# Low parts of the down-projection weights made by an accumulating DMA instead of a GpSimd subtraction

## The chip, the core and the metric

The kernel runs on one NeuronCore of a Trainium2 chip. The metric is the device time of one execution in microseconds (us); for several runs the median is given. TensorE is called PE, VectorE DVE, ScalarE ACT, GpSimd POOL or Pool, and SyncE, which issues the DMAs of before, SP.

## The reference

One layer of a hybrid diffusion backbone is computed for 512 latent tokens and 128 context tokens, 640 columns in all. The part that matters here is the last one, the down projection of the gated feed-forward network:

```python
f_gate, f_val = jnp.split(up, 2, axis=-1)
f = (jax.nn.silu(f_gate) * f_val) @ prm["w_ffn_down"]
x = x + g2 * rms_norm(f, prm["norm_ffn_post"])
```

`w_ffn_down` is 2816 x 1024 in float32. Ahead of it stand the mixing sub-layer (input projection, state-space scan, convolutions, output projection) and the up projection with its depthwise convolution.

## The kernel before

**Products in two parts.** A float32 product is made of three matmuls on rounded operands (fp32r). Each weight tile `raw` is split into a high part `hi`, which is `raw` rounded, and a low part `lo = raw - hi`; activations are split in the same way. `mm3` (L407 to L415) then adds hi x high, hi x low and lo x high. For each 128 x 128 block of weights PE so runs six matmuls, three products in two column halves of 384 and 256.

**Units.** The weights are cut into units of 128 x 1024 or less, one per load. `fetch` (L277) loads a unit with a DMA on SP's queue into `wr` (two buffers) and calls `split_unit` (L294). There the rounding `raw` to `wh` runs on ACT (L311) and the subtraction to `wl` on Pool or DVE (L313); `wh` and `wl` have three buffers each. So a unit's two parts can be written once PE is done with the unit three places earlier, and its raw buffer is free for the load two places later once the split has read it.

**The down projection.** Output block m (0 to 7, 128 rows each) needs three units g = 0, 1, 2 over the 2816 input rows; the third is 768 wide. `DOWN_ORDER` loads them as (0,0), (0,1), (1,0), (1,1), (0,2), (1,2), and from m = 2 on three by three: 24 units, called D0 to D23 in this order. Blocks 0 and 1 run interleaved, since the last activations are not yet there. Their splits (`split_act`, L397 to L404) go on at the same time: rounding on ACT (L400), subtraction on DVE or Pool (L402). The convolutions of the last up blocks on DVE (L1237 to L1240) and their gating product on Pool (L1339) run beside them. When a block is done, ACT squares and scales it (L1412, L1418) and Pool adds the square up (L1414). At the end the sums of squares give the norm, which is applied half by half on DVE and Pool (L1446, L1447) and stored.

**The order of the work.** The order in which each engine issues its instructions is written out by hand in the table `ORDER`, by positions in program order, and `issue_in_order` pins it. Engines issue strictly in that order and wait on semaphores, so a late operand holds up all that stands behind its reader on that engine. PE's order puts the first blocks of D2 among the last of D1.

Of the kernel before, what the change touches and what calls it, by code (L numbers as in the profile page):

```python
# [7 lines left out]
F32 = mybir.dt.float32  # L8
F32R = mybir.dt.float32r
AF = mybir.ActivationFunctionType  # L10
ALU = mybir.AluOpType
MUL, ADD, SUB, MAX, MIN = ALU.mult, ALU.add, ALU.subtract, ALU.max, ALU.min
# [25 lines left out]
for _name, _w in (("b_ada", 48), ("g_mix_pre", 8), ("g_mix_post", 8), ("g_ffn_pre", 8),  # L38
# [94 lines left out]
630 628-629 635 631 641 636-637 646 642 653 647-648 655 654 658 656-657 660 659 663 661-662 665 664 668  # L133
666-667 670 669 673 671 675 672 674 678 676 680 677 679 683 681 685 682 684 688 686 690 687 689 693 691 695
692 694 698 696 700 697 699 703 701 727 705 702 704 708 706 709 707 714 710-713 715 719 716 725-726 717 720
731 718 723 721-722 732 724 728-729 733-734 730 735 741 736-740 745 742-744 746-747 751 748-750 752-753 757
754-756 758-759 763 760-762 764-765 769 766-768 770-771 775 772-774 776-784""",
    "Pool": """
0-13 16-19 14-15 24-25 20 26-27 33 21-23 65 69 28-30 35 70 36 34 75 51 93 31 37-42 32 49 43 50 44-48 71 97
52-59 98 64 66 72 67 77 60 76 61 73 62-63 74 80 103-104 99 78-79 81-84 92 68 105 100 85-88 94 89 123 108 90  # L140
# [43 lines left out]
def hybrid_layer_kernel(ctx: ExitStack, tc: tile.TileContext, xT, ct, prm, cst, wrest, wdt, idhl_d, wada1, wada2, win,  # L184
                        wout, wup, wdown, st0, yT, nsf, nsb):
    nc = tc.nc
    te, ve, ac, gp, sy = nc.tensor, nc.vector, nc.scalar, nc.gpsimd, nc.sync
# [22 lines left out]
    def slot(tag, dt=F32, shape=(P, T)):  # L210
        if tag in ("H8", "T8"):
            return sb.tile([P, T + 64], dt, tag=tag, name=nm(tag))[:, 48:48 + shape[1]]
        return sb.tile(list(shape), dt, tag=tag, name=nm(tag))
# [55 lines left out]
    def add_unit(src, lo_eng=gp):  # L269
        units.append((src, lo_eng))  # L270
        return len(units) - 1
# [7 lines left out]
    def fetch(upto):  # L279
        if horizon[0] is not None:  # L280
            upto = min(upto, horizon[0])
        while cursor[0] < len(units) and cursor[0] <= upto:
            j = cursor[0]
            src, _ = units[j]
            n = src.shape[1]
            t = wp.tile([P, 1024], F32, tag="wr", name=f"wr{j}", bufs=2)
            sy.dma_start(t[:, :n], src)
            loaded[j] = t
            cursor[0] += 1
            split_unit(j)  # L290
# [5 lines left out]
    def split_unit(j):  # L296
        src, lo_eng = units[j]
        n = src.shape[1]
        raw = loaded.pop(j)
        if j in KEEP:  # L300
            parts = [[], []]
            for i, (c0, c1) in enumerate(((0, T), (T, n))):
                hi, lo = (slot(KEEP[j][2 * q + i], F32R, (P, c1 - c0)) for q in range(2))
                ac.activation(hi, raw[:, c0:c1], AF.Copy)
                lo_eng.tensor_tensor(lo, raw[:, c0:c1], hi.bitcast(F32), SUB)
                parts[0] += [hi[:, c:c + P] for c in range(0, c1 - c0, P)]
                parts[1] += [lo[:, c:c + P] for c in range(0, c1 - c0, P)]
            ready[j] = parts
            return
        hi = wp.tile([P, 1024], F32R, tag="wh", name=f"wh{j}")  # L310
        ac.activation(hi[:, :n], raw[:, :n], AF.Copy)  # L311
        lo = wp.tile([P, 1024], F32R, tag="wl", name=f"wl{j}")
        lo_eng.tensor_tensor(lo[:, :n], raw[:, :n], hi[:, :n].bitcast(F32), SUB)  # L313
        ready[j] = (hi, lo)


    unit_of = {}
# [70 lines left out]
    DOWN_ORDER = [(m, g) for gs in ((0, 1), (2,)) for m in range(2) for g in gs]  # L388
    DOWN_ORDER += [(m, g) for m in range(2, KD) for g in range(3)]
    for m, g in DOWN_ORDER:  # L390
        unit_of["down", m, g] = add_unit(wdown[m, :, 1024 * g:min(1024 * (g + 1), DFF)])


    split_ins = [None]
# [3 lines left out]
    def split_act(hi_tag, lo_tag, src, lo_eng):  # L398
        hi = slot(hi_tag, F32R)
        hi_ins[0] = ac.activation(hi, src, AF.Copy)  # L400
        lo = slot(lo_tag, F32R)
        split_ins[0] = lo_eng.tensor_tensor(lo, src, hi.bitcast(F32), SUB)  # L402
        return hi, lo
# [121 lines left out]
    for s in range(4):  # L525
# [6 lines left out]
        for k in (k0, k0 + 1):  # L532
# [3 lines left out]
            hi, lo = split_act(f"H{k}", f"H{8 + k}", xs_[k], ve)  # L536
# [390 lines left out]
    for it in seq:  # L927
        if it[0] == "proj":
            n = it[1]
# [7 lines left out]
            elif n[0] == "B":  # L937
                g = int(n[1:])
                bT[g] = slot("M2")
                conv3_silu(pt, 8 + g, bT[g])  # L940
            elif n[0] == "C":
                g = int(n[1:])
# [521 lines left out]
    m = KD - 1  # L1464
# [132 lines left out]
```

## Time and profile before

| what | us |
|---|---|
| median of 3 runs (lowest, highest) | 981.96 (980.89, 983.74) |
| span of the profiled execution, first to last instruction | 979.4 |
| PE busy | 944.5 |
| DVE busy | 686.9 |
| POOL busy | 577.9 |
| ACT busy | 471.3 |
| subtractions of weights on Pool (L313), 127 in all | 290.4 |
| roundings of weights on ACT (L311), 131 in all | 131.3 |

The profile is of one execution. Its span is 2.56 us below the median of the runs; the record gives no other time for that execution. Busy time is a sum over the span, whatever the engine held up. In the rows of the timeline the columns are start, length, engine, line, operation, output from inputs and count, and in brackets the idle time ahead of it with what ended it. A low part appears as `wl`, a high part as `wh`, a raw unit as `wr`. Rows that the prediction uses are shown there.

### The profile page before, as it was taken

To read this page: it belongs to the slowest core of one execution; us is meant where nothing else is said; L and a number is where in the kernel's file an instruction comes from. 1 tells how busy PE (TensorE), PEld (TensorE's weight loads), DVE (VectorE), ACT (ScalarE), POOL (GpSimd) and SP (SyncE) were. 2 spreads that over 40 slices of the span, in tenths; PEclk is the share of its full clock that TensorE was granted. 3 is DMA by queue.
4 is the path that set the end of the run, shared out by engine and by line. 5 is a ranking of instruction groups with operands and counts; after the bars stand their busy time and mean duration, and the time that the engine had idled before them with its cause. 6 is when DMAs were issued, how large, how long until landed. Compare 5 with 4: busy or idle time off the path is not lost.

```text
span 979.4 us, 18795 instructions
## 1 busy us (share of the span) xinstructions
PE 944.5 (96%) x7623; PEld 920.9 (94%) x7623; DVE 686.9 (70%) x1076; ACT 471.3 (48%) x799; POOL 577.9 (59%) x416
## 2 busy tenths in 40 slices
PE   4999999999999999999999999999999999999995
PEld 3799999999999998998889999999999999999995
DVE  1769898999989997523585998998988898400004
ACT  4355666877668477622464852323232336322211
POOL 1334699889999882534662994444454436543434
PEclk9999999999999999999999999999999999999998
DMA  9622424433424422578662322222222231322213
GB/s 347 250 72 86 117 82 127 146 95 123 139 80 142 128 91 93 196 244 303 200 218 88 129 86 69 84 78 73 86 66 86 66 87 54 94 69 76 82 38 108
DMA packets 50294, 117.52 MB, mean 120 GB/s; under 512 B 6016, under 2 KB 13952, under 8 KB 50208
## 3 DMA queue, kind: packets, MB, share of 16 engines
q1 hardware_dynamic: 50208, 116.33, 37.2%
q8 instruction: 60, 0.98, 0.4%
q14 instruction: 26, 0.21, 0.1%
HBM read 112.55 MB, written 3.75 MB: 119 GB/s over the span
## 4 chain that ended last, share of the span: by engine, by line
PE 87%; DMA 3%; ACT 3%; DVE 2%; SPq 1%; POOL 1%; issue 1%; POOLq 0%; ACTq 0%; DVEq 0%
PE ps L415 72%; PE ps L1259 3%; PE pq L415 2%; PE pq L818 2%; PE pq L807 1%; PE pq L460 1%; SPq L452 1%; DMA wr<-in_wout 1%; PE pq L744 1%; PE pq L441 1%; POOL wl L313 1%; PE pq L473 1%; DMA S<-acD 1%; ACT wh L311 1%; DMA T<-in_wada 1%
## 5 line engine op out<-in xcount | busy, mean ns | idle before, releaser
L313 POOL TENSOR_TENSOR wl<-wr,wh 128x1024 fp32r<-128x1024 f32 (+3 forms) x127 | 290.4, 2290 | 316.3 <-ACT wh L311 299.2
L415 PE MATMUL ps<-H,wh 128*128 128x384 f32 (+1 forms) x1636 | 315.7, 309 | 0.1
L311 ACT ACTIVATE wh<-wr 128x1024 fp32r<-128x1024 f32 (+3 forms) x131 | 131.3, 1003 | 316.2 <-PE ps L415 183.2
L415 PE MATMUL ps<-T,wh 128*128 128x384 f32 (+1 forms) x1472 | 272.5, 306 | 1.8 <-ACT S L1227 1.8
L1237 DVE SCALAR_TENSOR_TENSOR S<-ps,prms,S 128x441 f32<-128x441 f32 (+2 forms) x336 | 233.5, 695 | 29.4 <-ACT S L1227 18.9
L415 PEld LDWEIGHTS ps<-H,wh 128*128 128x128 f32 x1636 | 249.0, 188 | 2.7 <-issue 1.7
L415 PEld LDWEIGHTS ps<-T,wh 128*128 128x128 f32 x1472 | 218.9, 188 | 2.2 <-ACT S L1227 2.1
L872 DVE SCALAR_TENSOR_TENSOR ps<-u,prms,ps 128x655 f32<-128x655 f32 x205 | 185.1, 903 | 10.8 <-ACT ps L869 4.8
L415 PE MATMUL ps<-H,wl 128*128 128x384 f32 (+1 forms) x818 | 191.8, 309 | 0.0
L415 PE MATMUL ps<-T,wl 128*128 128x384 f32 (+1 forms) x736 | 166.2, 305 | 0.0
L415 PEld LDWEIGHTS ps<-H,wl 128*128 128x128 f32 x818 | 129.0, 188 | 1.0 <-issue 1.0
L415 PEld LDWEIGHTS ps<-T,wl 128*128 128x128 f32 x736 | 113.0, 188 | 0.0
L488 DVE RECIPROCAL rsm<-rsm 128x160 f32<-128x160 f32 (+2 forms) x9 | 7.4, 817 | 147.1 <-ACT rsm L487 147.1
L415 PE MATMUL ps<-S,wh 128*128 128x384 f32 (+1 forms) x420 | 88.0, 310 | 1.6 <-ACT wh L311 1.6
L415 PEld LDWEIGHTS ps<-S,wh 128*128 128x128 f32 x420 | 66.5, 188 | 2.8 <-ACT wh L311 1.8
L415 PE MATMUL ps<-S,wl 128*128 128x384 f32 (+1 forms) x210 | 54.9, 309 | 0.3 <-POOL wl L313 0.3
L789 ACT ACTIVATE S<-S,AC 128x128 f32<-128x128 f32 x140 | 45.5, 392 | 2.4 <-DMA S<-acD 2.4
L885 POOL TENSOR_TENSOR T<-T,T 128x640 f32<-128x640 f32 x20 | 32.0, 1602 | 12.5 <-ACT T L881 12.5
L1227 ACT ACTIVATE S<-ps,prms 128x640 f32<-128x640 f32 x42 | 36.5, 869 | 0.0
L415 PEld LDWEIGHTS ps<-S,wl 128*128 128x128 f32 x210 | 35.2, 188 | 0.9 <-POOL wl L313 0.5
L881 ACT ACTIVATE T<-u,prms 128x512 f32<-128x512 f32 (+1 forms) x54 | 27.9, 554 | 6.8 <-POOL T L885 6.8
L1339 POOL TENSOR_TENSOR H<-S,S 128x640 f32<-128x640 f32 x16 | 25.3, 1581 | 0.0
(346 smaller groups left out, 1180.3 us busy)
## 6 DMA issues: line engine op xcount, KB each, us to landing
wr<-in_wup SPq DMA_DIRECT2D x44, 512.0 KB, 3.5
wr<-in_win SPq DMA_DIRECT2D x36, 512.0 KB, 3.9
T<-in_wada SPq DMA_DIRECT2D x49, 256.0 KB, 5.4
S<-acD SPq DMA_DIRECT2D x28, 320.0 KB, 4.7
wr<-in_wdown SPq DMA_DIRECT2D x16, 512.0 KB, 3.4
wr<-in_wout SPq DMA_DIRECT2D x13, 512.0 KB, 4.5
H<-in_wada SPq DMA_DIRECT2D x23, 256.0 KB, 4.6
S<-in_wada SPq DMA_DIRECT2D x16, 256.0 KB, 5.4
```

The source lines that it names most:

```text
L311: ac.activation(hi[:, :n], raw[:, :n], AF.Copy)
L313: lo_eng.tensor_tensor(lo[:, :n], raw[:, :n], hi[:, :n].bitcast(F32), SUB)
L415: last_mm[0] = te.matmul(out, w, x[:, c0:c1], start=first and i == 0, stop=last and i == 2)
L789: ac.activation(rc, rc, AF.Relu, scale=-1.0, bias=AC2[:, c, row:row + 1])
L818: te.matmul(py[64 * h:64 * h + 64, i * P:(i + 1) * P], xt[:, c * P + 64 * h:c * P + 64 * h + 64], rs[h, d][:, c * P:(c + 1) * P], start=d ...
L872: ve.scalar_tensor_tensor(acc, u[:, j:j + UO], w(j), acc, MUL, ADD)
L881: ac.activation(t[:, b:c], u[:, a:a + c - b], AF.Copy, scale=w(j))
L885: gp.tensor_tensor(far, far, t, ADD)
L1227: ac.activation(out, v, AF.Identity, bias=prm_col("ffn_b", i), scale=w(1, 1))
L1237: ve.scalar_tensor_tensor(ob, vl[:, r0 + a - 1:r1 + a - 1, q0 + b - 1:q1 + b - 1], w(a, b), ob, MUL, ADD)
L1259: te.matmul(pt[:, o:o + c1 - c0], w[k] if i in (1, 2) else w[:, k * P:(k + 1) * P], x[:, c0:c1], start=k == 0 and j == 0, stop=k == KD - 1 ...
L1339: gp.tensor_tensor(f_raw[q], a, b, MUL)
```

## The change

For 22 of the 24 down units, all but D0 and D1, the low part is no longer a subtraction. ACT writes the negated rounding of the raw unit into `wl` (scale -1, output fp32r), and then a DMA issued from Pool's queue reads the raw weights from DRAM once more and adds them onto `wl` in place: -hi + raw. The high part, the raw load and PE's instructions stay as they are.

```diff
         lo = wp.tile([P, 1024], F32R, tag="wl", name=f"wl{j}")
-        lo_eng.tensor_tensor(lo[:, :n], raw[:, :n], hi[:, :n].bitcast(F32), SUB)
+        if j in ADDED:
+            ac.activation(lo[:, :n], raw[:, :n], AF.Copy, scale=-1.0)
+            gp.dma_start(lo[:, :n], src, accum_op=ADD)
+        else:
+            lo_eng.tensor_tensor(lo[:, :n], raw[:, :n], hi[:, :n].bitcast(F32), SUB)
         ready[j] = (hi, lo)
...
         unit_of["down", m, g] = add_unit(wdown[m, :, 1024 * g:min(1024 * (g + 1), DFF)])
+    ADDED = {unit_of["down", m, g] for m, g in DOWN_ORDER[2:]}
...
-731 718 723 721-722 732 724 728-729 733-734 730 735 741 736-740 745 742-744 746-747 751 748-750 752-753 757
+731-732 718 723 721-722 733-734 724 728-729 735-738 730 739-740 746-747 741-745 751-752 748-750 753-756
```

Of `ORDER` only ACT's list changes, where 22 instructions are put in; the last two lines of the diff are the place where that begins. The order of PE, DVE and SP is the same instruction by instruction.

ACT's queue around D2 and D3, before. Here `wh_9342` is the high part of D2 and `wr_9340` its raw unit, `wh_9396` that of D3; `T_814`, `H_820` and `H_822` are high parts of activations, `S_824` is the start of the last convolution and `S_807` the last gate:

```order
L311 ACTIVATE wh_9342<-wr_9340 128x1024
L400 ACTIVATE T_814_9275<-H_751_7890 128x640
L1227 ACTIVATE S_824_9295<-ps_798_9186,prms 128x640
L400 ACTIVATE H_820_9287<-H_766_8301 128x640
L400 ACTIVATE H_822_9291<-H_771_8438 128x640
L311 ACTIVATE wh_9396<-wr_9394 128x1024
L1333 ACTIVATE S_807_9251<-S_807_9251 128x640
```

The same place of ACT's queue with the change; `wl_9344` and `wl_9399` are the low parts of D2 and D3:

```order
L312 ACTIVATE wh_9342<-wr_9340 128x1024
L315 ACTIVATE wl_9344<-wr_9340 128x1024
L406 ACTIVATE T_814_9275<-H_751_7890 128x640
L1233 ACTIVATE S_824_9295<-ps_798_9186,prms 128x640
L406 ACTIVATE H_820_9287<-H_766_8301 128x640
L406 ACTIVATE H_822_9291<-H_771_8438 128x640
L312 ACTIVATE wh_9397<-wr_9395 128x1024
L315 ACTIVATE wl_9399<-wr_9395 128x1024
L1339 ACTIVATE S_807_9251<-S_807_9251 128x640
```

Each negated copy stands right behind the rounding of its unit, and everything behind it moves back by one instruction.

Pool's queue at the same place, before; `T_811`, `T_813` and `T_815` are low parts of activations, `S_825` is the last gating product, and `wl_9344`, `wl_9398`, `wl_9452`, `wl_9506`, `wl_9560` are the low parts of D2 to D6:

```order
L402 TENSOR_TENSOR T_811_9269<-H_737_7604,T_810_9267 128x640
L402 TENSOR_TENSOR T_813_9273<-H_746_7753,T_812_9271 128x640
L313 TENSOR_TENSOR wl_9344<-wr_9340,wh_9342 128x1024
L402 TENSOR_TENSOR T_815_9277<-H_751_7890,T_814_9275 128x640
L313 TENSOR_TENSOR wl_9398<-wr_9394,wh_9396 128x1024
L313 TENSOR_TENSOR wl_9452<-wr_9448,wh_9450 128x768
L1339 TENSOR_TENSOR S_825_9308<-S_807_9251,S_824_9295 128x640
L313 TENSOR_TENSOR wl_9506<-wr_9502,wh_9504 128x768
L313 TENSOR_TENSOR wl_9560<-wr_9556,wh_9558 128x1024
```

With the change:

```order
L408 TENSOR_TENSOR T_811_9269<-H_737_7604,T_810_9267 128x640
L408 TENSOR_TENSOR T_813_9273<-H_746_7753,T_812_9271 128x640
L316 DMA wl_9344<-in_wdown 128x1024
L408 TENSOR_TENSOR T_815_9277<-H_751_7890,T_814_9275 128x640
L316 DMA wl_9399<-in_wdown 128x1024
L316 DMA wl_9454<-in_wdown 128x768
L1345 TENSOR_TENSOR S_825_9308<-S_807_9251,S_824_9295 128x640
L316 DMA wl_9509<-in_wdown 128x768
L316 DMA wl_9564<-in_wdown 128x1024
```

Each subtraction is replaced by a DMA issue in the same place of the queue; nothing else on Pool moves. A DMA of this kind waits for ACT's negated copy, and the first matmul that reads the low part waits for the DMA where it waited for Pool.

More of the change, by code (lines that the diff above doesn't have):

```diff
@@ L135 @@
 692 694 698 696 700 697 699 703 701 727 705 702 704 708 706 709 707 714 710-713 715 719 716 725-726 717 720
-731 718 723 721-722 732 724 728-729 733-734 730 735 741 736-740 745 742-744 746-747 751 748-750 752-753 757
-754-756 758-759 763 760-762 764-765 769 766-768 770-771 775 772-774 776-784""",
+731-732 718 723 721-722 733-734 724 728-729 735-738 730 739-740 746-747 741-745 751-752 748-750 753-756
+760-761 757-759 762-765 769-770 766-768 771-774 778-779 775-777 780-783 787-788 784-786 789-792 796-797
+793-795 798-806""",
     "Pool": """
```

## The prediction

> **What bounds the kernel now.** I read the page first, then busy time by stage, then who waits for whom at the down projection, then the timelines of the four engines around the first changed unit. A change in the down units can only act on the stage that uses them, so the stages come before the totals.
>
> ```profile
> PE 944.5 (96%) x7623; PEld 920.9 (94%) x7623; DVE 686.9 (70%) x1076; ACT 471.3 (48%) x799; POOL 577.9 (59%) x416
> ...
> PE 87%; DMA 3%; ACT 3%; DVE 2%; SPq 1%; POOL 1%; issue 1%; POOLq 0%; ACTq 0%; DVEq 0%
> ```
>
> TensorE is busy in 96% of the span and carries 87% of the chain that ended last. The stages (columns: length; busy us of PE, PEld, DVE, ACT, POOL; granted clock; DMA share; GB/s):
>
> ```profile
> 806.00:846.00 40.00, 40.00 (x280) 40.00 (x279) 32.99 (x39) 19.86 (x27) 24.94 (x12) 1.00 0.23 68
> 846.00:962.00 116.00, 116.00 (x819) 115.72 (x818) 0.75 (x1) 29.54 (x44) 46.91 (x23) 1.00 0.23 66
> 962.00:979.40 17.40, 7.33 (x67) 6.83 (x65) 10.87 (x21) 2.01 (x6) 12.05 (x12) 0.78 0.43 152
> ```
>
> From 806 to 962 us, which is the whole down projection, PE has no idle time at a granted clock of 1.00. From 780 us to the end the view of waits, cut to PE, has only these, both in the tail behind the down units:
>
> ```profile
> PE pq L481 <- DVE rsm L488: 1.5, 1, 1.5
> PE pq L473 <- ACT AT L1412: 0.5, 1, 0.5
> ```
>
> So PE never waits for a low part here, and what the change removes from Pool cannot shorten the stage: its gain is 0. What remains is whether the new path delivers each low part before PE asks for it.
>
> **The change part by part.** I call the down units D0 to D23 in load order: (0,0), (0,1), (1,0), (1,1), (0,2), (1,2), (2,0), (2,1), (2,2), (3,0) and so on; those of the third column group are 768 wide. D2 to D23 are changed: 14 wide ones and 8 narrow ones.
>
> *Removed:* 22 Pool subtractions, from 806 to 962 us in these groups:
>
> ```profile
> L313 POOL TENSOR_TENSOR wl<-wr,wh 128x1024 fp32r<-128x1024 f32 x15 | 36.8, 2454 | 50.9 <-ACT wh L311 50.8
> L313 POOL TENSOR_TENSOR wl<-wr,wh 128x768 fp32r<-128x768 f32 x8 | 15.5, 1933 | 19.9 <-ACT wh L311 19.9
> ```
>
> 14 x 2.45 + 8 x 1.93 = 49.8 us of Pool work go, all of it beside a full PE: 0 us.
>
> *Added on ACT:* 22 negated copies of the shape of the rounding, 1.05 us wide and 0.85 us narrow (rows below), 14 x 1.05 + 8 x 0.85 = 21.5 us on an engine that is busy for 29.54 of 116 us. The cover is ACT's idle time; it is missing only where ACT is full, and that is at D2:
>
> ```profile
> 818.71 1.05 ACT L311 ACTIVATE wh<-wr 128x1024 fp32r<-128x1024 f32 x1
> 819.66 0.72 ACT L400 ACTIVATE T<-H 128x640 fp32r<-128x640 f32 x1
> 820.29 0.87 ACT L1227 ACTIVATE S<-ps,prms 128x640 f32<-128x640 f32 x1
> 821.06 1.36 ACT L400 ACTIVATE H<-H 128x640 fp32r<-128x640 f32 x2
> ```
>
> The negated copy stands right behind the rounding of D2, so it runs from 819.66 to 819.66 + 1.05 = 820.71, and the three rows behind it come 0.95 us later. The DVE shows whether that hurts:
>
> ```profile
> 821.32 7.49 DVE L402 TENSOR_TENSOR H<-H,H 128x640 fp32r<-128x640 f32 x4
> 828.73 5.80 DVE L1237 SCALAR_TENSOR_TENSOR S<-ps,prms,S 128x441 f32<-128x441 f32 x8
> ```
>
> The last convolution starts at 828.73, and its seed (ACT at 820.29) would be written at 822.1: 6.6 us to spare. The split halves that ACT delays (821.06) feed the third and fourth of the four DVE operations. Cost 0.
>
> *Added on Pool:* 22 DMA issues in the places of the subtractions. D2's stands between three activation splits and a fourth:
>
> ```profile
> 815.12 4.71 POOL L402 TENSOR_TENSOR T<-H,T 128x640 fp32r<-128x640 f32 x3 [3.03 <-ACT T L400]
> 819.89 2.42 POOL L313 TENSOR_TENSOR wl<-wr,wh 128x1024 fp32r<-128x1024 f32 x1
> 822.26 2.17 POOL L402 TENSOR_TENSOR T<-H,T 128x640 fp32r<-128x640 f32 x1
> ```
>
> Pool is free at 819.83, before the copy is done at 820.71, so Pool's queue adds no wait. The fourth split waits behind the issue as it did behind the subtraction. Now the reader of D2's low part, in PE's queue:
>
> ```profile
> 822.84 0.62 PE L415 MATMUL ps<-S,wh 128*128 128x384 f32 x3
> ...
> 824.16 0.27 PE L415 MATMUL ps<-S,wh 128*128 128x256 f32 x1
> 824.27 0.46 PE L415 MATMUL ps<-S,wl 128*128 128x384 f32 x2
> ```
>
> Before, the low part is ready at 819.89 + 2.42 = 822.31, and PE reads it at 824.27: 1.96 us of slack. Afterwards it is ready at 820.71 + L, where L runs from the end of the negated copy to the landing of the accumulating DMA. PE's queue is in order and every later matmul stands behind this one, so the whole kernel slips by 820.71 + L - 824.27 = **L - 3.56 us**. Nothing gives it back, since PE is full to 962 us.
>
> *L* has no row: before, no DMA is issued from Pool. The nearest rows (queue, count, KB each, median us to landing, then SP's own time for an issue in ns and the landing's minimum, median and maximum):
>
> ```profile
> wr<-in_wdown SPq DMA_DIRECT2D x16, 512.0 KB, 3.4
> ...
> wr<-in_wdown SPq DMA_DIRECT2D x8, 384.0 KB, 3.1
> ...
> H<-acD SPq DMA_DIRECT2D x4, 320.0 KB, 5.8
> ```
>
> ```profile
> L287 SPq DMA_DIRECT2D wr<-in_wdown x24: 327/328/328, 789.9 to 938.1; - x24
> ...
> DMA to landing us min/median/max: 3.0/3.4/4.1
> ```
>
> - the plain load of the same weights: 3.4 us;
> - the accumulation also has to fetch what lies in wl: one more 512 KB, at (3.4 - 3.1) us per 128 KB = 1.2 us;
> - the end of the same copy also frees the raw buffer, so SP loads D4 (384 KB) in the same moments: 3 x 0.3 = 0.9 us of shared engines;
> - Pool's own issue, between SP's 0.33 us and the 2.42 us of the subtraction in its place: I take the middle, 1.4 us.
>
> L = 3.4 + 1.2 + 0.9 + 1.4 = 6.9 us, and the stall at D2 is 6.9 - 3.56 = **3.3 us**. Low end: the fastest landing and SP's issue, 3.0 + 0.33 = 3.3 us, below 3.56: no stall. High end: the slowest load row of a similar size, 5.8, with the other terms at their highest, 5.8 + 1.2 + 0.9 + 2.4 = 10.3 us: 6.8 us at D2.
>
> [...]
>
> *Later units.* A buffer is freed three units earlier, so they have more room. The tightest, D6, and the first of the regular ones, D9 (rounding on ACT, then PE's first read of the low part):
>
> ```profile
> 841.83 1.04 ACT L311 ACTIVATE wh<-wr 128x1024 fp32r<-128x1024 f32 x1
> ...
> 859.00 1.06 ACT L311 ACTIVATE wh<-wr 128x1024 fp32r<-128x1024 f32 x1 [4.89 <-PE ps L415]
> ```
>
> ```profile
> 852.44 0.45 PE L415 MATMUL ps<-S,wl 128*128 128x384 f32 x2
> ```
>
> ```profile
> 871.40 0.45 PE L415 MATMUL ps<-S,wl 128*128 128x384 f32 x2
> ```
>
> With 2.0 us for the two ACT passes, D6 has 852.44 - 841.83 - 2.0 = 8.6 us for L, D9 has 871.40 - 859.00 - 2.0 = 10.4. At L = 6.9 neither stalls; at 10.3, D6 adds 1.7 us. Pool's sums of squares (six in the stage) stand in the queue where they stood and keep the same waits.
>
> **Sum.** The span of 979.4 plus 3.3 is 982.7 us. The median of the runs, 981.96, lies 2.6 us above the profiled span; with that, the forecast is **985.3 us**, 0.34% slower. About 0.3%, 2.95 us here, is what a measurement of this kernel can tell from no change; that is L = 6.5 us.
>
> **The rivals.**
>
> *Quick landing (0.37), no change to be measured.* If L stays under 6.5, the stall is 0 to 2.9 us: 982.0 to 984.9, around 983.5. For it: the down loads land within 3.0 to 4.1 us, and the stage's DMA share is 0.23, so there is room. Against it: it needs the second fetch, the neighbour load and Pool's issue together to stay under 3.1 us over the plain 3.4.
>
> *The accumulating DMA is slow by itself (0.12), slower by far.* If adding in flight stretches L past 10.4 us, the buffer ring no longer covers it and every output block pays. The deciding point is D9's room. At L = 12: 8.4 at D2, 3.4 at D6, then 1.6 in each of the five blocks 3 to 7, 8.0; together 19.8 us, 1001.8. No row speaks for such a rate, and none excludes it.
>
> *VectorE holds Pool's issue back (0.05), slower.* Pool and DVE disturb each other here:
>
> ```profile
> L402 DVE TENSOR_TENSOR H<-H,H x5: 812/2198/3032, 821.3 to 835.8; 128x640 fp32r<-128x640 f32 x5
> ```
>
> The same DVE subtraction takes 812 or 3032 ns. If the issue had to wait until the four at 821.32 are through (4 x 0.81 us undisturbed, to 824.6), L counts from there: 824.6 + 6.9 - 3.56 - 820.71 = 7.2 us, 989.2. [...]
>
> *Faster (0.04).* No wait of PE on a low part exists in the stage to be removed, and the order of instructions shows 22 real DMA issues, so the change does what it says. What is left is the spread of the runs, 980.89 to 983.74.
>
> **How the numbers follow.** The forecast, one stall of 2.9 to about 8.5 us, has 0.42. Slower by over 0.3%: 0.42 + 0.12 + 0.05 = 0.59; within 0.3%: 0.37; faster: 0.04. The range starts at 981.5 (no stall, less the spread) and ends at 991.0, just above the high end of L (979.4 + 6.8 + 1.7 + 2.6 = 990.5). It leaves out the slow accumulation (0.12) above and some 0.08 below.
>
> **What would show it.** In the profile after: one PE wait of about 3 us near 824 us on the DMA that writes wl, no other PE wait up to the tail, PE matmul time unchanged, Pool's subtractions down by 22 and its issues landing in about 7 us. No such wait would speak for the quick landing; waits at D6 and in every block from 3 on for the slow accumulation; an issue on Pool that begins only when the DVE run ends for the third. The prediction is wrong if the stage gets shorter, or if PE first waits elsewhere.

## The result and the profile after

The kernel with the change takes 988.88 us (median of 4 runs, 987.49 to 989.71); the kernel before, run beside it, 982.85 us (4 runs, 980.89 to 984.12). The ratio is 1.0063 with a 95% interval of 1.0045 to 1.0080: 6.2 us slower, between 4.4 and 7.9. Forecast were 985.3 us, between 981.5 and 991.0, and 3.3 us of loss.

The profiled execution after took 989.71 us, with a span of 987.9. From its page, the busy times:

```profile
PE 948.0 (96%) x7623; PEld 923.7 (94%) x7623; DVE 681.8 (69%) x1076; ACT 490.4 (50%) x821; POOL 545.0 (55%) x416
```

ACT is busy for 19.1 us more, the 22 copies, and Pool for 32.9 us less, the subtractions against the issues; neither is what the time shows. By stage (columns as in the prediction: length; busy us of PE, PEld, DVE, ACT, POOL; granted clock; DMA share; GB/s):

```profile
806.00:846.00 40.00, 36.65 (x246) 36.45 (x245) 30.05 (x44) 22.16 (x30) 16.95 (x12) 0.96 0.41 92
846.00:970.00 124.00, 124.00 (x874) 123.72 (x873) 1.02 (x2) 46.33 (x63) 25.16 (x24) 1.00 0.67 141
```

Before, the first of these stages had 40.00 us of PE at a clock of 1.00. Now 3.35 us of PE are missing in it, and the clock is 0.96; the second stage is full at 1.00 as before. The view of waits, PE alone, from 780 to 990 us, names the one new wait, beside the two of the tail that were there before:

```profile
PE ps L421 <- DMA wl<-in_wdown: 3.3, 1, 3.3
```

The three timelines around it, ACT with D2's negated copy, then Pool with D2's issue, then PE:

```profile
823.13 1.04 ACT L315 ACTIVATE wl<-wr 128x1024 fp32r<-128x1024 f32 x1
```

```profile
824.82 1.04 POOL L316 DMA_DIRECT2D wl<-in_wdown  x1 [1.51 <-ACT T L406]
```

```profile
827.64 0.27 PE L421 MATMUL ps<-S,wh 128*128 128x256 f32 x1
831.26 0.90 PE L421 MATMUL ps<-S,wl 128*128 128x384 f32 x2 [3.35 <-DMA wl<-in_wdown]
831.96 1.27 PE L421 MATMUL ps<-S,wh 128*128 128x384 f32 x4
...
833.56 1.06 PE L421 MATMUL ps<-S,wh 128*128 128x384 f32 x4
834.46 0.45 PE L421 MATMUL ps<-S,wl 128*128 128x384 f32 x2
834.74 0.73 PE L421 MATMUL ps<-S,wh 128*128 128x384 f32 x4
835.32 0.45 PE L421 MATMUL ps<-S,wl 128*128 128x384 f32 x2
```

The negated copy ends at 824.17, Pool's instruction starts at 824.82, and PE goes on at 831.26: from the copy to PE it is 7.1 us, against 3.56 that D2 had. Behind the wait six matmuls take 833.56 - 831.96 = 1.60 us instead of 835.32 - 834.46 = 0.86 a little later. The clock in steps of 2 us says why:

```profile
828.00:830.00 2.00, 0.00 (x0) 0.00 (x0) 2.00 (x4) 2.00 (x4) 0.71 (x1) 1.00 1.02 184
830.00:832.00 2.00, 0.74 (x3) 0.74 (x4) 1.89 (x4) 0.61 (x1) 0.16 (x1) 0.71 1.04 254
832.00:834.00 2.00, 2.00 (x9) 2.00 (x9) 1.90 (x4) 0.00 (x0) 0.00 (x0) 0.50 0.83 152
834.00:836.00 2.00, 2.00 (x15) 2.00 (x14) 1.93 (x5) 0.00 (x0) 0.00 (x0) 0.94 0.40 78
```

The granted clock is 0.50 from about 830.8 to 834.2. The 14 matmuls from 831.26 to 834.74 took 3.48 us; at 0.86 us for six they take 2.0. So the wait of 3.35 us brought 1.5 us of slow matmuls with it, 4.85 us in all.

The two profiled spans differ by 979.4 to 987.9, 8.5 us, more than that. The last matmul ahead of the wait shows the rest: it starts at 824.16 before and at 827.64 after, 3.48 us later, and up to D2's copy the queues hold the same instructions in the same order in both kernels. That part is not the change's. Almost half of it lies at 458.8 us, far ahead of the down projection, where the granted clock fell in the profiled execution of after and did not in that of before. The same stretch, before and then after:

```profile
458.00:463.00 5.00, 5.00 (x70) 4.54 (x62) 3.23 (x3) 2.05 (x4) 2.65 (x2) 1.00 0.81 277
```

```profile
458.00:463.00 5.00, 4.79 (x77) 4.12 (x78) 2.10 (x2) 2.16 (x4) 1.57 (x1) 0.66 0.90 293
```

That is 5.0 x 0.34 = 1.7 us of clock. Another 1.47 us lie between 22 and 30 us, where the clock of after was at 0.50 from 25.28 to 28.69 us (1.00 in the same stretch before) and PE waited 0.98 us for a DMA in place of 0.41: the matmul `pq<-csts,adar` at 22.23 us starts 0.02 us ahead of the same one at 22.25 before, the next of its kind at 29.94 us 1.45 behind that at 28.49. Some 0.3 us are left for small differences between the two executions. From the matmuls at 824.16 and 827.64 on, 8.5 - 3.48 = 5.0 us are left for the change. The 3.35 us in brackets is PE's idle time. The first matmul on D2's low part starts 0.11 us after the one ahead of it before and 3.62 us after it now, so it slips by 3.51 us, and with the 1.5 us of the clock that is the 5.0.

How the new DMAs land, from the page (queue, count, KB each, median us):

```profile
wr<-in_wdown SPq DMA_DIRECT2D x16, 512.0 KB, 4.0
wl<-in_wdown POOLq DMA_DIRECT2D x14, 512.0 KB, 7.3
```

and by the line that issues them (duration of Pool's instruction in ns, then the landing's minimum, median and maximum):

```profile
L316 POOL DMA_DIRECT2D wl<-in_wdown x22: 853/864/1037, 824.8 to 957.0; - x22
...
DMA to landing us min/median/max: 4.9/6.8/7.7
```

D2's is the only one issued from 824 to 828 us and took 6.4 us. The last wide one, from 948 to 956 us, with no raw load beside it, took 5.5. The two rows:

```profile
wl<-in_wdown POOLq DMA_DIRECT2D x1, 512.0 KB, 6.4
```

```profile
wl<-in_wdown POOLq DMA_DIRECT2D x1, 512.0 KB, 5.5
```

### The profile page after: what moved, and what is told of

Same layout as the page of the kernel before. It is cut to its first block, busy times and chain, and to the rows that moved or that the text cites. A ratio compares the mean times of both kernels' runs of the same rounds, so it can differ in the third digit from the quotient of the medians.

```text
span 987.9 us, 18835 instructions
## 1 busy us (share of the span) xinstructions
PE 948.0 (96%) x7623; PEld 923.7 (94%) x7623; DVE 681.8 (69%) x1076; ACT 490.4 (50%) x821; POOL 545.0 (55%) x416
## 3 DMA queue, kind: packets, MB, share of 16 engines
q0 software_dynamic: 3168, 10.49, 6.0%
HBM read 123.04 MB, written 3.75 MB: 128 GB/s over the span
## 4 chain that ended last, share of the span: by engine, by line
PE 86%; DMA 5%; ACT 3%; DVE 2%; SPq 1%; POOL 1%; issue 1%; POOLq 0%; ACTq 0%; DVEq 0%
PE ps L421 72%; PE ps L1265 3%; DMA T<-in_wada 2%; PE pq L824 2%; PE pq L813 1%; PE pq L421 1%; PE pq L466 1%; DMA wr<-in_wout 1%; PE pq L750 1%; DMA S<-acD 1%; SPq L458 1%; PE pq L447 1%; ACT wh L312 1%; DMA S<-in_wada 1%; DMA wl<-in_wdown 1%
## 5 line engine op out<-in xcount | busy, mean ns | idle before, releaser
L318 POOL TENSOR_TENSOR wl<-wr,wh 128x1024 fp32r<-128x1024 f32 (+3 forms) x105 | 240.3, 2292 | 252.3 <-ACT wh L312 224.0
L316 POOL DMA_DIRECT2D wl<-in_wdown x22 | 19.3, 875 | 104.1 <-ACT wl L315 102.6
```

Of the source, the lines that this page charges most:

```text
L316: gp.dma_start(lo[:, :n], src, accum_op=ADD)
```

## The experiments

Two theories stood against each other at first. **A**: the whole loss comes from D2, the one unit whose low part was needed 3.56 us after its copy, and consists of the wait and of the slow matmuls behind it. **B**: the 22 units have a common cost (DMA traffic, ACT's copies, matmuls disturbed by writes into `wl`) of which D2's wait is only a part. A third, **C**, concerned the slow matmuls alone: the accumulating DMA disturbs PE, and not the pause.

### Only D2 back to a subtraction (d2_back)

```diff
-    ADDED = {unit_of["down", m, g] for m, g in DOWN_ORDER[2:]}
+    ADDED = {unit_of["down", m, g] for m, g in DOWN_ORDER[3:]}
```

> The change without D2: its low part is a Pool subtraction again, D3 to D23 keep the accumulating DMA. Theory A (the whole loss sits at D2: a PE wait of 3.35 us and then about 1.7 us because the granted clock is at 0.50 for some 3.4 us): the time of the kernel before, 982.9 us within 1.5, and no PE wait of over 0.5 us between 806 us and the tail. Rival B (the part of the 6.0 us beyond the forecast 3.3 us comes from the 22 DMAs as a whole, by shared DMA engines or by the new queue): 1 to 3 us above the kernel before, 984 to 986.

982.23 us against 981.88 for the kernel before; ratio 0.9997 (0.9987 to 1.0007). ACT's list in `ORDER` loses the one copy. PE waits from 780 us to the end, all of them:

```profile
PE pq L487 <- DVE rsm L494: 1.5, 1, 1.5
PE pq L479 <- ACT AT L1418: 0.5, 1, 0.5
```

21 of the 22 changed units together cost between -1.3 and 0.7 us. Theory B falls.

### Only D2 changed (d2_only)

```diff
-    ADDED = {unit_of["down", m, g] for m, g in DOWN_ORDER[2:]}
+    ADDED = {unit_of["down", m, g] for m, g in DOWN_ORDER[2:3]}
```

> D2 alone by the accumulating DMA, the other 23 down units by subtraction as before. Theory A: a PE wait of about 3.3 us at D2, a granted clock of 0.5 for about 3.4 us behind it, and 5 us over the kernel before, about 988. Rival B: only the forecast 3.3 us, about 986, since 21 of the 22 DMAs are gone. If the landing of 6.4 us at D2 is made by D2's own neighbours (the raw load of D4 beside it), it stays at 6.4.

986.52 us; ratio 1.0048 (1.0031 to 1.0065), a loss of 4.7 us (3.0 to 6.4). PE's timeline has the wait again, and slow matmuls again, from 1.3 us behind it:

```profile
828.29 0.56 PE L420 MATMUL ps<-S,wl 128*128 128x384 f32 x2 [3.50 <-DMA wl<-in_wdown]
...
829.59 1.27 PE L420 MATMUL ps<-S,wh 128*128 128x384 f32 x4
...
832.79 0.52 PE L420 MATMUL pq<-T,wh 128*128 128x384 f32 x2
```

The 20 matmuls from 828.29 to 832.79 took 4.5 us, at 0.86 for six 2.9: 1.6 us lost to the clock. With the wait of 3.50 that makes 5.1, inside the interval. One unit of 22 carries the loss; that the whole change measures 1.5 us more than this run is within the two intervals.

### D2's copy and DMA earlier (d2_early)

The change, with D2's two ACT passes put three activation splits earlier in ACT's queue, the copy first, and its DMA issue ahead of one more activation split on Pool. Of the order, ACT's and Pool's lists at the place:

```diff
-... 710-713 715 719 716 725-726 717 720 731-732 718 ...
+... 710-713 715 719 716 725 732 731 726 717 720 718 ...
-... 364 367-369 372 370 373-374 ...
+... 364 367-368 372 369-370 373-374 ...
```

> The whole change, with D2's two ACT passes two activation roundings earlier (the negated copy first, then the rounding) and its DMA ahead of the third activation split on Pool. Theory A: the copy ends about 2.8 us earlier, some 6.4 us before PE's read; with 7.0 us from the end of the copy to the landing PE waits 0.6 us, too short for a change of the clock, and the time is 983.5, within 0.3% of the kernel before. Rival B: the common cost of 1 to 3 us stays on top, 984.5 to 986.5. If ACT's later roundings or Pool's later splits become the new wait, PE waits on them instead between 820 and 830 us.

983.01 us; ratio 1.0006 (0.9989 to 1.0022). The wait shrinks, and the six matmuls behind it keep their pace, 824.81 - 823.95 = 0.86 us:

```profile
823.55 0.56 PE L421 MATMUL ps<-S,wl 128*128 128x384 f32 x2 [0.72 <-DMA wl<-in_wdown]
823.95 0.74 PE L421 MATMUL ps<-S,wh 128*128 128x384 f32 x4
...
824.81 0.73 PE L421 MATMUL ps<-S,wh 128*128 128x384 f32 x4
```

The time is that of the kernel before within the interval, so an earlier start of D2 takes the loss away. It brings the kernel back to the time of before, not under it, as PE had no wait there to lose.

### The same DMAs without the addition (plain)

The low part of the 22 units is the raw weight here, without the rounding taken off; the negated copy is still made, and overwritten.

```diff
-            gp.dma_start(lo[:, :n], src, accum_op=ADD)
+            gp.dma_start(lo[:, :n], src)
```

> The same DMAs from Pool without the addition, so the low part is the raw weights and not the remainder; the second read of wl is left out. By the forecast's term of 1.2 us for fetching wl, D2's landing is 5.2 us instead of 6.4, the PE wait about 2.1 us instead of 3.35, and the median landing of the wide units falls from 7.3 to about 6.1. If adding costs nothing beside Pool's own path, the landings stay where they are; if it costs half of the transfer, they fall to 4.

One execution, 985.79 us, too few for a verdict; its trace counts here. The wait is 1.69 us and no slow matmul follows:

```profile
828.25 0.56 PE L421 MATMUL ps<-S,wl 128*128 128x384 f32 x2 [1.69 <-DMA wl<-in_wdown]
828.65 0.73 PE L421 MATMUL ps<-S,wh 128*128 128x384 f32 x4
...
829.51 0.73 PE L421 MATMUL ps<-S,wh 128*128 128x384 f32 x4
```

The DMA view from 800 to 975 us gives the price of the addition. First the change (packets, MB and time as a share of 16 engines):

```profile
q0 software_dynamic: 3168, 10.49, 34.1%
```

then without the addition, with Pool's own instruction from the view of the line:

```profile
q0 software_dynamic: 3168, 10.49, 17.2%
...
wl<-in_wdown POOLq DMA_DIRECT2D x14, 512.0 KB, 4.2
```

```profile
L316 POOL DMA_DIRECT2D wl<-in_wdown x22: 527/530/754, 823.5 to 952.6; - x22
```

The same packets and bytes took the DMA engines twice as long when they were added, 34.1% against 17.2% of the stretch, a wide unit landed in 7.3 instead of 4.2 us, and Pool's instruction took 0.86 instead of 0.53. At D2, whose unit landed in 6.4 us in the change, the addition was worth 3.35 - 1.69 = 1.7 us. The forecast's 1.2 us for it was too little in both places: what came out is the outcome named last, landings of about 4 us. The forecast had put it on one more fetch of 512 KB, as its author's estimate; no run here tells a fetch from the adding.

### A late low part without any DMA (late2, late3)

The kernel before, with D2's subtraction made three and four times on Pool. If the pause slows PE, its matmuls are slow here too; if the accumulating DMA does it, they are not.

```diff
-        lo_eng.tensor_tensor(lo[:, :n], raw[:, :n], hi[:, :n].bitcast(F32), SUB)
+        for _ in range(3 if j == unit_of.get(("down", 1, 0)) else 1):
+            lo_eng.tensor_tensor(lo[:, :n], raw[:, :n], hi[:, :n].bitcast(F32), SUB)
```

> The kernel before, with D2's subtraction made three times over by Pool instead of once; no DMA is added. The low part is ready 2 x 2.42 = 4.8 us later, so PE waits 2.9 us at D2 (1.96 us of slack). Theory A2 (the clock falls when PE has stood idle long enough, between 1.7 us, where it did not, and 3.35 us, where it did): either outcome places the limit; with no fall 2.9 us over the kernel before, with one 4.6. Rival C (the accumulating DMA itself slows the matmuls that read its buffer): granted clock 1.00 behind the wait.

> As the last one with the subtraction made four times: ready 7.3 us later, a PE wait of 5.3 us. Theory A2: granted clock about 0.5 for some 3.4 us behind the wait, 1.7 us lost there, 7.0 us over the kernel before in all, without any DMA on Pool. Rival C: full clock at once, 5.3 us over the kernel before.

late2: 988.65 us against 982.64; ratio 1.0061 (1.0039 to 1.0084). Pool's three passes, PE's wait, and the clock in late2:

```profile
822.92 8.25 POOL L314 TENSOR_TENSOR wl<-wr,wh 128x1024 fp32r<-128x1024 f32 x3
```

```profile
831.22 0.56 PE L416 MATMUL ps<-S,wl 128*128 128x384 f32 x2 [3.75 <-POOL wl L314]
```

```profile
831.00:832.00 1.00, 0.78 (x5) 0.78 (x6) 0.85 (x1) 0.12 (x1) 1.00 (x2) 0.91 0.00 0
832.00:835.00 3.00, 3.00 (x13) 3.00 (x13) 1.70 (x1) 0.62 (x1) 3.00 (x2) 0.50 0.46 131
835.00:836.00 1.00, 1.00 (x8) 1.00 (x7) 1.00 (x1) 0.00 (x0) 0.60 (x1) 0.88 0.00 0
```

late3: 991.68 us; ratio 1.0099 (1.0068 to 1.0131), with a wait of 6.62 us. Its clock falls while PE still waits and no DMA runs (share 0.00), and is down until behind 835:

```profile
828.00:829.00 1.00, 0.00 (x0) 0.00 (x0) 0.92 (x1) 0.04 (x1) 0.92 (x2) 0.83 0.00 0
829.00:831.00 2.00, 0.00 (x0) 0.00 (x0) 0.00 (x0) 0.69 (x1) 2.00 (x1) 0.50 0.00 0
...
835.00:836.00 1.00, 1.00 (x7) 1.00 (x6) 1.00 (x2) 0.00 (x0) 0.00 (x0) 0.75 0.06 12
```

No accumulating DMA is in either kernel, so theory C falls: a pause of PE alone, of 3.75 and of 6.62 us, was enough for the fall of the clock. Both waits came out longer than expected, since the three passes took 8.25 us, 2.75 each instead of 2.42, and late3's four 11.12, 2.78 each. late2's sum is 3.75 and 1.7 of clock (0.78 x 0.09 + 3.0 x 0.5 + 0.12), 5.4 us, against 6.0 measured (3.8 to 8.3). In late3 the 20 matmuls behind the wait, from 831.17 to 836.15, took 4.98 us instead of 2.9, so 2.1 us of clock; with the wait that is 8.7 us, against the 9.0 by which the medians differ.

### All 24 units changed (all24)

```diff
-    ADDED = {unit_of["down", m, g] for m, g in DOWN_ORDER[2:]}
+    ADDED = {unit_of["down", m, g] for m, g in DOWN_ORDER}
```

> All 24 down units by the accumulating DMA, D0 and D1 too. By the formula of the forecast with the measured 7.0 us from the end of the copy to the landing: D0's copy ends 2.0 us after its rounding starts (800.05 in the trace of before), it lands at 809.1, and PE reads it at 807.6: a new wait of 1.5 us at D0, with the clock left at 1.00. D1 is read 12 us after its copy: no wait. D2 waits 3.35 us as in the change and loses 1.7 us by the clock. 1.5 us over the change, about 6.5 over the kernel before. If the landing depended on the place rather than on the path, D0 would not wait.

992.08 us; ratio 1.0088 (1.0061 to 1.0115). PE's waits on low parts from 780 us on, D2's and D0's:

```profile
PE ps L421 <- DMA wl<-in_wdown: 4.1, 1, 4.1
PE pq L421 <- DMA wl<-in_wdown: 2.0, 1, 2.0
```

The clock behind D0's wait of 2.05 us (ended at 812.09), and behind D2's of 4.06 (ended at 833.09):

```profile
812.00:813.00 1.00, 0.91 (x6) 0.91 (x7) 0.00 (x0) 0.67 (x1) 1.00 (x2) 1.00 0.78 111
...
834.00:835.00 1.00, 1.00 (x6) 1.00 (x5) 0.93 (x3) 0.00 (x0) 0.00 (x0) 0.59 1.04 217
835.00:837.00 2.00, 2.00 (x10) 2.00 (x9) 1.93 (x5) 0.00 (x0) 0.00 (x0) 0.50 0.29 56
837.00:838.00 1.00, 1.00 (x7) 1.00 (x6) 1.00 (x2) 0.00 (x0) 0.00 (x0) 0.71 0.00 0
```

One kernel shows both cases: a wait of 2.05 us costs itself, and one of 4.06 costs 0.41 + 1.0 + 0.29 = 1.7 us of slow matmuls besides. Leaving D0 and D1 out of the change saved D0's 2 us.

## Why the prediction was right or wrong

**Place and sign** were right. PE's first wait is at D2's low part, on the DMA that writes `wl`, once, and no other unit waits; D2 alone makes up the loss (d2_only), and without it there is none (d2_back). The 0 us for the removed subtractions, for ACT's copies and for Pool's queue hold: d2_back has all of them but one.

**The stall** was forecast at 3.3 us and measured at 3.35 of idle time, 3.5 of slip. L was to be 6.9 us and was 7.1 at D2. Pool's own part was put at 1.4, the middle between 0.33 and 2.42, and was 0.65 from the copy to the instruction and 1.04 for the instruction, 1.7 (the landing counts from its beginning). The addition was put at 1.2 and was worth 1.7 at D2, of which up to 0.3 is Pool's longer instruction. The neighbour load (0.9) can be judged by the end of the queue: the last wide unit landed in 5.5 us, D2 in 6.4, of which 0.2 can be D2's longer instruction. Nothing more than these two rows shows it. So the terms were off by some tenths of a us in both directions, and that the sum came within 0.2 us, with a middle value in it, is in part luck. In the regular wide units the addition cost 7.3 - 4.2 = 3.1 us, far more than 1.2, but D6 and the later ones had 8.6 us and more of room for it. The high end's 10.3 - 3.56 is 6.7 and not 6.8; nothing hangs on it.

**The step that failed** is the sum: "979.4 plus 3.3 is 982.7", on the premise "PE matmul time unchanged". The granted clock was quoted at 1.00 in the stage, and nothing was counted for what a pause of PE does to it. Behind a wait of 3.35 us the clock stood at 0.50, which cost 1.5 us in the change (1.6 to 1.7 in d2_only, late2 and at D2 of all24). The slip and the clock make 5.0 us, inside the measured 4.4 to 7.9; forecast were 3.3 us. The 1.2 us between 5.0 and the middle of the interval have no cause that the runs show. The time of 988.88 us lies inside the forecast range all the same, but that is luck: the upper part of the range was meant for a slower landing, not for a slower clock. Of the 3.6 us above the forecast, 0.9 is the kernel before, which measured 982.85 in place of 981.96.

The averages over all executions agree with the two parts. The nine of d2_only have a mean span of 984.77 us at a mean clock of 0.9930, the 26 of the kernel before beside them 980.12 at 0.9941: 4.65 us more, of which 984.77 x 0.0070 - 980.12 x 0.0059 = 1.1 us is an estimate of the lost clock, and 3.5 is the wait. In late2 it is 6.2 us, of which 2.4 clock, and 3.8 the wait.

**The rivals.** *Quick landing* needed L under 6.5; it was 7.1. Without the addition it would have held: a wait of 1.69, no clock loss. *Slow accumulation* needed L over 10.4; the slowest landing of the 22 is 7.7. *VectorE holding Pool's issue* fell: D2's issue began 0.65 us behind the copy and took 1.04 us, while DVE was in its four subtractions; the median of all issues is 0.86. The 0.18 us more is not DVE's either. In all24, where D0's issue is the first, that one takes 1.04 us and D2's, with DVE busy for 0.96 and 1.00 of the two microseconds from 825 to 827 in which it lies, 0.87.

```profile
824.79 4.84 DVE L408 TENSOR_TENSOR H<-H,H 128x640 fp32r<-128x640 f32 x4
```

**Left open.** No fixed length divides the waits of PE with a lower clock from those without. At D2 and D0 the clock fell during or behind all five waits of 3.35 us and more, and not behind 0.72, 1.69 and 2.05 us. But before, after and all24 each have a wait of 1.76 us on ACT near 543 us, and in all24 the mean clock of the 4 us behind it was 0.57, where it was 1.00 in the other two (before: 542.49 to 546.49). All24, the wait and the 4 us from its end:

```profile
543.47 0.92 PE L421 MATMUL ps<-T,wh 128*128 128x384 f32 x4 [1.76 <-ACT S L1233]
```

```profile
543.47:547.47 4.00, 4.00 (x17) 4.00 (x18) 3.82 (x6) 3.98 (x7) 4.00 (x4) 0.57 0.74 272
```

The same wait and stretch after, in the change:

```profile
545.97 0.82 PE L421 MATMUL ps<-T,wh 128*128 128x384 f32 x4 [1.76 <-ACT S L1233]
```

```profile
545.97:549.97 4.00, 4.00 (x27) 4.00 (x28) 3.82 (x6) 3.98 (x7) 4.00 (x4) 1.00 0.71 262
```

Whether another execution of the change escapes the slow clock is therefore open; each kernel has one trace. D2's DMA cut in two halves, the first of which would land earlier, was not tried. No version was faster than the kernel before, which agrees with a PE that has no wait in this stage to lose.

## What to carry to other kernels

An operation on an idle engine that is replaced by a DMA costs its latency at the one reader with the least slack (7.1 us against 3.56 at D2): work out that slack for every unit, above all where the work of two stages overlaps. Count an accumulating DMA as it was measured here: twice the DMA engines' time of a plain one (34.1% against 17.2%), plus the issuing engine's instruction (0.86 us) and the hand-over from the producer (0.65 us at D2). And price a pause of PE in a dense stage above its length: waits of 3.35 to 4.06 us cost 1.5 to 1.7 us more here, one of 6.62 us 2.1, and those of 0.72, 1.69 and 2.05 us nothing more; in all24 a slow clock stood behind one of 1.76 us too. Or move the producer a few instructions earlier, which here took the whole loss away.

## What the runs showed of the hardware that was not expected

- The granted clock fell to 0.50 and came back to 1.00 in one piece. Read from the windows it was down for 3.4 us in the change (830.8 to 834.2), in d2_only, in late2 and at D2 of all24, and for 6.8 us in late3, twice that. It fell 2.9 to 5.2 us after PE had stopped. In late2, all24 and d2_only PE had by then been at work again for 0.6, 1.1 and 1.2 us.
- In the change the clock fell at 25.28, 458.78, 830.83 and 981.02 us. These are 433.50, 372.05 and 150.19 us apart: 127, 109 and 44 times 3.413, and 3.41 us is also how long each of the first three lasted. The trace of before has one fall, near 971.9 us, and so no distance to set beside these.
- PE's busy time just ahead of a fall does not settle it. In the five traces with a long wait at D2, PE was busy for at most 1.2 of the 3.4 us ahead of the fall, 0.49 in the change. But ahead of the falls at 25.28 and 458.78 us in the change it was busy for 1.67 and 1.65 of 3.41 us, and from 544.11 to 547.52 us for 1.65 as well, with the clock at 1.00 in it and behind it up to 549.97.
- The accumulating DMAs took the DMA engines twice the time of plain ones for the same 3168 packets, 34.1% against 17.2% of the stretch from 800 to 975 us.
- VectorE's four subtractions at D2 took 4.84 us after, with Pool busy for 3.00 of them, and 7.49 us before, with Pool busy for 6.07. PE did not wait for them in either.
